# Rotary's loads in GpSimd's queue, and two of the constants' pieces at a time

## The chip, the cores and the metric

The kernel runs on one core of a Trainium2 chip. The metric is the device time in microseconds of one execution, as the median of the runs. The core has the tensor engine (PE, with its weight loads as PEld), the Vector engine (DVE), the Scalar engine (ACT), GpSimd (POOL) and the sync engine (SP). SP, ACT and GpSimd issue DMA transfers, each into a queue of its own.

## What is computed

A decoder trunk of two layers over 1024 tokens of width 1024. Each layer has two mixers beside each other: windowed attention with partial rotary, and a gated linear recurrence (HGRN2). Their outputs are gated, added, projected and added to the stream. Cut to what the change touches:

```python
for layer in range(DEPTH):                     # 2
    h = rms_norm(x, norm_w[layer])
    proj = h @ w_in[layer]                     # (1024, 1024) @ (1024, IN_WIDTH)
    (q, k, v, z_attn, q_h, f_h, i_h, g_h, gate_attn, gate_hgrn) = split(proj)
    q = partial_rope(q.reshape(B, T, 8, 64), positions)    # the first 16 of each head's 64
    k = partial_rope(k.reshape(B, T, 2, 64), positions)
    a = sliding_window_attention(q, k, v, sinks) * silu(z_attn)
    ...                                        # HGRN2: b
    x = x + (sigmoid(gate_attn) * (a @ w_up_attn) + sigmoid(gate_hgrn) * (b @ w_up_hgrn)) @ w_out
return rms_norm(x, final_norm_w)
```

`partial_rope` turns pairs of columns: `x1*cos - x2*sin, x2*cos + x1*sin`. Everything is fp32.

## The kernel before

**Precision and products.** Each fp32 operand is split into a high and a low part. ACT rounds the high part (`whi`, L130, `wh`, L290), the Vector engine subtracts it for the low part (`wlo`, L131, `wl`, L291). A product is three matmuls (lo x hi, hi x lo, hi x hi): L296, L297, L298.

**Pairs.** The columns of `w_in` are worked off in 15 *pairs* m = 0 to 14 (loop at L638, `pair` at L274), each two 128-column blocks, with a Strassen-Winograd scheme that needs seven products of half blocks instead of eight. A pair loads its two weight halves `wr_m_0` and `wr_m_1` (512 KB each, L87, on SP's queue; in the profile both are called `wr`). The Vector engine makes sums and differences from them (`ws`, L282, L283, L285, L286), and ACT and the Vector engine split these (suffixes `_s`, `_t` and, for the first product, `_a`).

PE then does groups of 12 matmuls into two accumulators `pb` and `pc`: `pb` with `_s`, `pc` with `_s`, `pb` with `_t`, `pc` with `_t`, and at the end `pb` with `wl`/`wh`. For the pairs up to 11 (layer 0) or 10 (layer 1) the first product was made earlier; the others have two more groups, with `_a`, in front. Between the groups the Vector engine reads the accumulators out (L307): `pq_12<-pb`, `pq_22<-pc`, `pq_22<-pb`, `pq_12<-pc`, `pq_21<-pb`. The last group overwrites `pb`, so it waits until the third of these, `pq_22<-pb`, has run.

**Weight buffers.** The pool `wraw` has two buffers, so `wr_{m+1}_0` can be issued only after L286 of pair m, the last reader of the first half, and `wr_{m+1}_1` only after L291 of pair m.

**Rotary.** The generator `rotary()` turns five tiles of 128 rows, the keys (n = 0, j = 0) and four of queries (j = 1, 2, 4, 5). It is stepped by `use`, a callback in `pair`, from pair 9 (`TURN`) on. At its first step it loads the tables `cosT` and `sinT` (L604). Each tile is loaded as `y` (512 KB, L610) and once more with the halves of the rotary columns exchanged, as `other` (4 x 32 KB, L615; one buffer for all tiles). Then `y*cos` (L617), `other*sin` (L619), the sum (L620), ACT's high part `yh` (L623) and the low part (L625). GpSimd stores the parts: `ksd` for the keys (8 x 256 KB, L629 and L630), `qsd` for each tile of queries (4 x 256 KB, L633 and L634).

**The constants.** `constants()` makes the rotary tables in four pieces (`tab`, L479 to L493: short steps on the Vector engine, four PE transposes, an ACT copy `tabo` and a store from ACT's queue into `tabs`); `next(consts, None)` at the end of each pair makes one step.

**What sets the order.** Each engine has a queue that it works off in order. A scheduler sets these orders when the kernel is built, from the order of the code and from estimates; on the chip they are fixed. A row behind a waiting one waits too.

Of the kernel before, what the change touches and what calls it, by code (L numbers as in the profile page):

```python
# [28 lines left out]
HALF = 8  # L29
# [11 lines left out]
def trunk_kernel(ctx, tc, x, positions, norm_w, w_in, attn_sinks, hgrn_norm_w, w_up_attn,  # L41
                 w_up_hgrn, w_out, lb_logits, final_norm_w, c_ident, c_side, c_upper, c_diag, c_lev,
                 c_freq, out):
    nc = tc.nc
# [12 lines left out]
    def slot(shape, name, dt=F32):  # L57
        return sp.tile(shape, dt, tag="slot", name=name)
# [330 lines left out]
    tabs = [dp.tile([P, T], F32, name=f"tabs_{i}") for i in range(2)]  # L389
# [115 lines left out]
    consts = constants()  # L505


    for L in range(DEPTH):
# [5 lines left out]
        yd = [dp.tile([P, T], F32, name=f"yd_{L}_{j}") for j in range(6)]  # L514
# [85 lines left out]

        def rotary():
            cosT, sinT = (slot([P, T], f"{n}T_{L}") for n in ("cos", "sin"))
            for t, d in zip((cosT, sinT), tabs):
                nc.sync.dma_start(t, d)  # L604

            o = slot([P, T], f"other_{L}")
            G.memset(o, 0.0)
            for n, j in enumerate((0, 1, 2, 4, 5)):
                y = slot([P, T], f"y_{L}_{j}")
                nc.sync.dma_start(y, yd[j])  # L610
                for r in range(2):
                    for i in range(2):
                        a = r * HD + i * HALF
                        b = r * HD + (1 - i) * HALF
                        nc.sync.dma_start(o[a:a + HALF], yd[j][b:b + HALF])  # L615
                yield
                V.tensor_tensor(out=y, in0=y, in1=cosT, op=ALU.mult)  # L617
                yield
                V.tensor_tensor(out=o, in0=o, in1=sinT, op=ALU.mult)  # L619
                V.tensor_tensor(out=y, in0=y, in1=o, op=ALU.add)  # L620
                yield
                hi = slot([P, T], f"yh_{L}_{j}", F32R)
                S.copy(hi, y)  # L623
                lo = y.bitcast(F32R)
                V.tensor_tensor(out=lo, in0=y, in1=hi.bitcast(F32), op=ALU.subtract)  # L625
                if n == 0:
                    for g, (own, far) in enumerate(((LO, HI), (HI, LO))):
                        for d, u in ((ksd[g][1 - g], (hi, lo)), (ksd[g][g], (lo, hi))):
                            nc.gpsimd.dma_start(d[own], u[0][own].bitcast(F32))  # L629
                            nc.gpsimd.dma_start(d[far], u[1][own].bitcast(F32))  # L630
                else:
                    for d, own, far in ((qsd[n - 1][0], LO, HI), (qsd[n - 1][1], HI, LO)):
                        nc.gpsimd.dma_start(d[own], hi[own].bitcast(F32))  # L633
                        nc.gpsimd.dma_start(d[far], lo[own].bitcast(F32))  # L634
                yield

        turning = rotary()
        for m in range(NPAIR):  # L638
            (c0, r0), (c1, r1) = pairs[m]

            def use(j, a, src, own):
                result(m, *pairs[m][j], a * 512, src, src if own else None)
                if m >= TURN:
                    next(turning, None)
            pair(wi, (c0, c1), parts, hT, f"{L}_{m}", p1s[m] if m < ahead else None, use)
            next(consts, None)
            if m == NPAIR - 2:
                vT, vn = slot([P, T], f"vT_{L}"), [slot([P, NB, P], f"vn_{L}")]
                nc.sync.dma_start(vT, yd[3])
# [470 lines left out]
        for m in range(0, KT, 2):  # L1120
# [5 lines left out]
            for a in range(2):  # L1126
                u, t = u2s[m // 2][a]
# [83 lines left out]
        m = split_a(a11, "s2")  # L1211
# [4 lines left out]
        m = split_a(a21, "s1")  # L1216
# [8 lines left out]
        m = split_a(a12, "s4")  # L1225
# [4 lines left out]
        m = split_a(a11, "s3")  # L1230
# [63 lines left out]
```

## Time and profile before

| | |
|---|---|
| median of 3 runs | 1426.08 us (1421.89 to 1428.8) |
| the profiled execution, its own time | 1425.17 us |
| its span | 1423.4 us |
| PE busy | 1389.6 us (98%) |
| Vector engine busy | 998.8 us (70%) |
| ACT busy | 694.4 us (49%) |
| GpSimd busy | 83.1 us (6%) |
| mean DMA rate | 169 GB/s |

Pair 9, with which rotary begins, starts its matmuls at about 219 us in layer 0 and 911 us in layer 1. A row of a timeline gives start and duration in us, engine, line, operation, output<-input and count; in brackets stands the idle time before and what ended it. A row of the waits view gives what waited, for what, the sum in us, how often and the longest. A row of a window gives each engine's busy time, the granted clock of PE, the share of the DMA engines and GB/s.

### The profile page before, as it was taken

What the parts mean: (1) busy time and instruction counts of PE and PEld (TensorE: products, weight loads), DVE (VectorE), ACT (ScalarE), POOL (GpSimd) and SP (SyncE); (2) the same over time, 40 slices, a digit from 0 to 9 for tenths busy, and PEclk for the clock granted to TensorE, in tenths of its full rate; (3) what the DMA queues carried; (4) which work ended last, traced back from release to release, by engine and by line L of the source; (5) the groups of instructions that cost most, each with busy time, mean ns of one, the idle gap of its engine ahead of it and who ended that gap; (6) DMA issues with size and microseconds to landing.
All of it is one profiled execution on the core that took longest, in us unless ns stands there. A gap on an engine that the chain in (4) does not pass through costs nothing.

```text
span 1423.4 us, 21284 instructions
## 1 busy us (share of the span) xinstructions
PE 1389.6 (98%) x8108; PEld 1125.5 (79%) x8108; DVE 998.8 (70%) x1638; ACT 694.4 (49%) x1386; POOL 83.1 (6%) x141
## 2 busy tenths in 40 slices
PE   8999999999999999999999999989999999999997
PEld 7888777778777787888878788868887778788885
DVE  6867667752755779589976565776347378876998
ACT  8753424343884555313576332334448746443244
POOL 1100001120000001000010000010200000100000
PEclk9999999999999999999999999999999999999999
DMA  9433446787134652671255344576933366329303
GB/s 276 156 126 126 140 156 201 248 268 270 60 119 159 231 189 90 244 264 54 74 198 165 106 130 142 194 222 202 320 123 97 133 213 217 120 62 401 129 0 119
DMA packets 203639, 240.05 MB, mean 169 GB/s; under 512 B 13648, under 2 KB 140112, under 8 KB 203536
## 3 DMA queue, kind: packets, MB, share of 16 engines
q1 hardware_dynamic: 159184, 153.73, 32.8%
q10 hardware_dynamic: 34944, 52.44, 10.2%
q0 software_dynamic: 9408, 32.51, 7.2%
q8 instruction: 64, 1.05, 0.3%
q14 instruction: 39, 0.32, 0.1%
HBM read 160.00 MB, written 78.64 MB: 168 GB/s over the span
## 4 chain that ended last, share of the span: by engine, by line
PE 79%; DVE 8%; DMA 5%; ACT 4%; issue 2%; SPq 1%; ACTq 0%; DVEq 0%
PE pb L296 5%; PE pb L297 5%; PE pb L298 5%; DMA wr<-in_w_in_dram 4%; PE pc L296 3%; PE pc L297 3%; PE pc L298 3%; PE pg L265 2%; PE pg L267 2%; PE pg L266 2%; PE pj_qh L141 2%; PE pj_qh L142 2%; PE av L762 2%; PE pj_qh L143 2%; PE pi L789 2%; PE pi L788 2%
## 5 line engine op out<-in xcount | busy, mean ns | idle before, releaser
L130 ACT CAST whi_s<-ws 128x1024 fp32r<-128x1024 f32 x30 | 31.6, 1052 | 139.6 <-DVE ws L283 120.5
L130 ACT CAST whi_o<-wo 128x1024 fp32r<-128x1024 f32 x20 | 21.1, 1054 | 77.0 <-PE pu_uh L143 35.5
L282 DVE TENSOR_TENSOR ws<-wr 128x512 f32<-128x512 f32 x30 | 20.7, 690 | 52.7 <-DMA wr<-in_w_in_dram 52.7
L532 ACT ACTIVATE pq<-pq 128x512 f32<-128x512 f32 x60 | 37.8, 630 | 31.8 <-DVE pq L307 26.1
L296 PE MATMUL pb<-th,wl 128*128 128x512 f32 x120 | 48.6, 405 | 4.4 <-DVE pq L307 4.3
L141 PE MATMUL pu_ua<-wh_a,wlo_ua 128*128 128x512 f32 x128 | 52.4, 409 | 0.0
L307 DVE TENSOR_TENSOR pq<-pb,p 128x512 f32<-128x512 f32 x46 | 31.7, 689 | 29.2 <-PE pb L298 29.1
L296 PE MATMUL pb<-th,wlo_s 128*128 128x512 f32 x120 | 48.0, 400 | 3.5 <-DVE y L617 3.2
L265 PE MATMUL pg<-hh,wl_p 128*128 128x512 f32 (+1 forms) x128 | 47.8, 375 | 3.0 <-ACT p L269 2.9
L143 PE MATMUL pu_ua<-wh_a,whi_ua 128*128 128x512 f32 x128 | 50.5, 395 | 0.0
L142 PE MATMUL pu_ua<-wl_a,whi_ua 128*128 128x512 f32 x128 | 50.4, 394 | 0.0
L143 PE MATMUL pu_uh<-wh_b,whi_uh 128*128 128x512 f32 x128 | 49.8, 389 | 0.0
L141 PE MATMUL pu_uh<-wh_b,wlo_uh 128*128 128x512 f32 x128 | 49.8, 389 | 0.0
L142 PE MATMUL pu_uh<-wl_b,whi_uh 128*128 128x512 f32 x128 | 49.8, 389 | 0.0
L737 ACT ACTIVATE pr<-pr,mx 128x128 f32<-128x128 f32 x128 | 49.7, 393 | 0.0
L296 PE MATMUL pb<-th,wlo_t 128*128 128x512 f32 x120 | 47.3, 394 | 2.1 <-DVE wlo_t L131 2.1
L296 PE MATMUL pc<-hh,wlo_t 128*128 128x512 f32 x120 | 47.9, 400 | 0.1
L131 DVE TENSOR_TENSOR wlo_t<-ws,whi_t 128x1024 fp32r<-128x1024 f32 x30 | 36.7, 1223 | 15.9 <-ACT whi_t L130 15.9
L297 PE MATMUL pb<-tl,wh 128*128 128x512 f32 x120 | 47.7, 398 | 0.0
L298 PE MATMUL pb<-th,wh 128*128 128x512 f32 x120 | 47.7, 398 | 0.0
L297 PE MATMUL pb<-tl,whi_s 128*128 128x512 f32 x120 | 47.4, 395 | 0.0
L297 PE MATMUL pb<-tl,whi_t 128*128 128x512 f32 x120 | 47.4, 395 | 0.0
(419 smaller groups left out, 4419.1 us busy)
## 6 DMA issues: line engine op xcount, KB each, us to landing
wr<-in_w_in_dram SPq DMA_DIRECT2D x72, 512.0 KB
gd<-pq ACTq DMA_DIRECT2D x79, 256.0 KB
fq<-fq ACTq DMA_DIRECT2D x48, 256.0 KB
wr_p<-in_w_in_dram SPq DMA_DIRECT2D x23, 512.0 KB
x<-in_x_dram SPq DMA_DIRECT2D x16, 512.0 KB
qs<-qsd POOLq DMA_DIRECT2D x16, 512.0 KB, 8.1
u<-gd SPq DMA_DIRECT2D x16, 512.0 KB
ga<-gd SPq DMA_DIRECT2D x16, 512.0 KB
```

The lines of the kernel that those rows point to most:

```text
L130: S.copy(hi, raw)
L131: eng.tensor_tensor(out=lo, in0=raw, in1=hi.bitcast(F32), op=ALU.subtract)
L141: PE.matmul(acc, lhsT=ll, rhs=rh, start=i == 0, stop=False)
L142: PE.matmul(acc, lhsT=lh, rhs=rl, start=False, stop=False)
L143: PE.matmul(acc, lhsT=lh, rhs=rh, start=False, stop=i == n - 1)
L265: PE.matmul(acc, lhsT=wl[:, k], rhs=h[:, t], start=k == 0, stop=False, skip_group_check=q > 0)
L296: PE.matmul(acc, lhsT=wl[:, k], rhs=h, start=start and k == 0, stop=False, skip_group_check=not start)
L297: PE.matmul(acc, lhsT=wh[:, k], rhs=l, start=False, stop=False, skip_group_check=not start)
L298: PE.matmul(acc, lhsT=wh[:, k], rhs=h, start=False, stop=k == 3, skip_group_check=not start)
L307: V.tensor_tensor(out=out, in0=in0, in1=in1, op=ALU.add)
L532: S.activation(d, src, AF.Sigmoid if r < 2 * KT else AF.Silu)
L737: S.activation(pr[:, h], pr[:, h], AF.Exp, bias=mx[:, h:h + 1], accum_out=sm[:, h:h + 1])
```

## The change

Rotary's loads (the tables, `y` and `other`) are issued by GpSimd instead of SP. Each tile's loads stand in the code ahead of the last tile's stores: the new inner function `load` is called for tile 0 before the loop, and for the next tile after the current one's sum. And after pairs 0 and 1 the constants are stepped twice instead of once.

```diff
         def rotary():
             cosT, sinT = (slot([P, T], f"{n}T_{L}") for n in ("cos", "sin"))
-            for t, d in zip((cosT, sinT), tabs):
-                nc.sync.dma_start(t, d)
 
             o = slot([P, T], f"other_{L}")
             G.memset(o, 0.0)
-            for n, j in enumerate((0, 1, 2, 4, 5)):
+
+            def load(j):
                 y = slot([P, T], f"y_{L}_{j}")
-                nc.sync.dma_start(y, yd[j])
+                nc.gpsimd.dma_start(y, yd[j])
                 for r in range(2):
                     for i in range(2):
                         a = r * HD + i * HALF
                         b = r * HD + (1 - i) * HALF
-                        nc.sync.dma_start(o[a:a + HALF], yd[j][b:b + HALF])
+                        nc.gpsimd.dma_start(o[a:a + HALF], yd[j][b:b + HALF])
+                return y
+
+            tiles = (0, 1, 2, 4, 5)
+            for t, d in zip((cosT, sinT), tabs):
+                nc.gpsimd.dma_start(t, d)
+            nxt = load(0)
+            for n, j in enumerate(tiles):
+                y = nxt
                 yield
                 V.tensor_tensor(out=y, in0=y, in1=cosT, op=ALU.mult)
                 yield
                 V.tensor_tensor(out=o, in0=o, in1=sinT, op=ALU.mult)
                 V.tensor_tensor(out=y, in0=y, in1=o, op=ALU.add)
+                if n < 4:
+                    nxt = load(tiles[n + 1])
                 yield
...
             pair(wi, (c0, c1), parts, hT, f"{L}_{m}", p1s[m] if m < ahead else None, use)
-            next(consts, None)
+            for _ in range(1 if m > 1 else 2):
+                next(consts, None)
```

In the changed file the lines are shifted: the loads of the tables are L619, `y` L609, `other` L614, the Vector engine's steps L624, L626, L627 and L634, the stores L638/L639 (`ksd`) and L642/L643 (`qsd`).

In GpSimd's queue, layer 0, this stands before behind the clearing of `other`:

```order
L607 MEMSET other_2123 128x1024
L629 DMA ksd_0_1_161<-yh_0_2232 64x1024
L630 DMA ksd_0_1_161<-y_0_2125 64x1024
L629 DMA ksd_0_0_160<-y_0_2125 64x1024
L630 DMA ksd_0_0_160<-yh_0_2232 64x1024
```

And this after the change:

```order
L605 MEMSET other_2121 128x1024
L619 DMA cosT_2119<-tabs_136 128x1024
L619 DMA sinT_2120<-tabs_137 128x1024
L609 DMA y_0_2125<-yd_0_139 128x1024
L614 DMA other_2121<-yd_0_139 8x1024 x4
L609 DMA y_1_2165<-yd_1_140 128x1024
L614 DMA other_2121<-yd_1_140 8x1024 x4
L638 DMA ksd_0_1_161<-yh_0_2238 64x1024
L639 DMA ksd_0_1_161<-y_0_2125 64x1024
```

The tables and two tiles stand ahead of the first store; each later tile's loads stand ahead of a group of stores.

On the Vector engine, layer 0, from the third readout of pair 9 (`pq_9_22<-pb`) on, before (`y_0` is the tile of keys):

```order
L307 TENSOR_TENSOR pq_9_22_2102<-pb_9_2074,pq_9_22_2102 128x512
L286 TENSOR_TENSOR ws_10_1_2170<-wr_10_0_2165,ws_10_0_2169 128x512
L131 TENSOR_TENSOR wlo_10_s<-ws_10_0_2169,whi_10_s 128x1024
L617 TENSOR_TENSOR y_0_2125<-y_0_2125,cosT_2119 128x1024
L307 TENSOR_TENSOR pq_9_12_2088<-pc_9_2075,pq_9_12_2088 128x512
L131 TENSOR_TENSOR wlo_10_t<-ws_10_1_2170,whi_10_t 128x1024
L307 TENSOR_TENSOR pq_9_21_2159<-pb_9_2074,p_0_8_901 128x512
L291 TENSOR_TENSOR wl_10_2184<-wr_10_1_2167,wh_10_2183 128x512
L619 TENSOR_TENSOR other_2123<-other_2123,sinT_2120 128x1024
```

And after:

```order
L626 TENSOR_TENSOR other_2121<-other_2121,sinT_2120 128x1024
L307 TENSOR_TENSOR pq_9_22_2102<-pb_9_2074,pq_9_22_2102 128x512
L627 TENSOR_TENSOR y_0_2125<-y_0_2125,other_2121 128x1024
L131 TENSOR_TENSOR wlo_10_s<-ws_10_0_2175,whi_10_s 128x1024
L307 TENSOR_TENSOR pq_9_12_2088<-pc_9_2075,pq_9_12_2088 128x512
L286 TENSOR_TENSOR ws_10_1_2176<-wr_10_0_2171,ws_10_0_2175 128x512
L634 TENSOR_TENSOR y_0_2125<-y_0_2125,yh_0_2238 128x1024
L307 TENSOR_TENSOR pq_9_21_2159<-pb_9_2074,p_0_8_901 128x512
L131 TENSOR_TENSOR wlo_10_t<-ws_10_1_2176,whi_10_t 128x1024
L291 TENSOR_TENSOR wl_10_2190<-wr_10_1_2173,wh_10_2189 128x512
```

The keys' rotation, of which only the product with cos stood in this stretch, is now finished in it, its low part (L634) included. `wl_10` is the last reader of `wr_10_1`, so `wr_11_1` follows it.

On the Vector engine, layer 1, around the readout of pair 10 that frees `pb`, before:

```order
L307 TENSOR_TENSOR pq_10_22_8144<-pc_10_8117,p_1_10_7069 128x512
L131 TENSOR_TENSOR wlo_11_a<-wr_11_0_8210,whi_11_a 128x1024
L307 TENSOR_TENSOR pq_10_22_8144<-pb_10_8116,pq_10_22_8144 128x512
L282 TENSOR_TENSOR ws_11_0_8214<-wr_11_1_8212 128x512
L285 TENSOR_TENSOR ws_11_1_8215<-wr_11_0_8210,wr_11_1_8212 128x512
```

And after:

```order
L307 TENSOR_TENSOR pq_10_22_8150<-pc_10_8123,p_1_10_7069 128x512
L131 TENSOR_TENSOR wlo_11_a<-wr_11_0_8210,whi_11_a 128x1024
L282 TENSOR_TENSOR ws_11_0_8214<-wr_11_1_8212 128x512
L307 TENSOR_TENSOR pq_10_22_8150<-pb_10_8122,pq_10_22_8150 128x512
L283 TENSOR_TENSOR ws_11_0_8214<-ws_11_0_8214,wr_11_0_8210 128x512
```

L282, the first reader of `wr_11_1`, now stands ahead of that readout. In layer 0 it stood ahead of it before too (`ws_11_0<-wr_11_1`, then `pq_10_22<-pb`); there L285 has joined it:

```order
L282 TENSOR_TENSOR ws_11_0_2285<-wr_11_1_2283 128x512
L285 TENSOR_TENSOR ws_11_1_2286<-wr_11_0_2281,wr_11_1_2283 128x512
L307 TENSOR_TENSOR pq_10_22_2221<-pb_10_2193,pq_10_22_2221 128x512
L283 TENSOR_TENSOR ws_11_0_2285<-ws_11_0_2285,wr_11_0_2281 128x512
L627 TENSOR_TENSOR y_1_2165<-y_1_2165,other_2121 128x1024
```

These are rows of the changed kernel, whose second tile (`y_1`) is summed right behind.

## The prediction

> **What bounds the kernel now.** The page's first part, the busy time of each engine, comes first:
>
> ```profile
> PE 1389.6 (98%) x8108; PEld 1125.5 (79%) x8108; DVE 998.8 (70%) x1638; ACT 694.4 (49%) x1386; POOL 83.1 (6%) x141
> ```
>
> TensorE (PE) is at work for 1389.6 of 1423.4 us, and the change takes no matmul away. So it can give back only idle PE time and time at a lowered clock. The waits view, for PE and for the tiles of a weight pair, says how much of that there is and who causes it:
>
> ```profile
> PE pb L296 <- DVE pq L307: 4.3, 4, 3.0
> PE pb L296 <- DVE y L617: 3.2, 1, 3.2
> PE pb L296 <- DVE wlo_t L131: 2.1, 1, 2.1
> DVE ws L282 <- DMA wr<-in_w_in_dram: 52.7, 20, 5.6
> ```
>
> Three waits of PE, of 3.0, 3.2 and 2.1 us, are single ones at L296, a matmul of a pair. PE's timeline has each (idle before in brackets), and with it the pitch that follows:
>
> ```profile
> 261.86 0.80 PE L296 MATMUL pb<-th,wl 128*128 128x512 f32 x1 [3.05 <-DVE pq L307]
> 262.45 0.63 PE L297 MATMUL pb<-tl,wh 128*128 128x512 f32 x1
> 262.88 0.63 PE L298 MATMUL pb<-th,wh 128*128 128x512 f32 x1
> ...
> 267.93 0.39 PE L298 MATMUL pb<-hh,whi_a 128*128 128x512 f32 x1
> 268.15 0.39 PE L296 MATMUL pb<-hh,wlo_a 128*128 128x512 f32 x1
> ```
> ```profile
> 946.86 0.63 PE L296 MATMUL pb<-th,wlo_s 128*128 128x512 f32 x1 [3.17 <-DVE y L617]
> ...
> 951.08 0.39 PE L298 MATMUL pb<-th,whi_s 128*128 128x512 f32 x1
> ```
> ```profile
> 956.31 0.47 PE L296 MATMUL pb<-th,wlo_t 128*128 128x512 f32 x1 [2.12 <-DVE wlo_t L131]
> ```
> ```profile
> 260.00:270.00 10.00, 8.14 (x24) 6.47 (x25) 9.66 (x13) 4.71 (x6) 0.00 (x0) 0.66 0.55 193
> ```
>
> After 3.05 us idle the matmuls start 0.43 us apart (262.45, 262.88) instead of 0.22 (267.93, 268.15), until 267.93: the last row, a 10-us window, has a granted clock of 0.66 (the number before 0.55). 14 matmuls took 6.07 us (261.86 to 267.93) instead of 14 x 0.227 = 3.18, so this stall cost 3.05 + 2.9 = 6.0 us. After 946.86 there are 11 matmuls in 4.22 us instead of 2.5: 3.17 + 1.7 = 4.9 us. The third, of 2.12 us, I take with 1.2 of slow clock, less than the second's 1.7: 3.3. All three lie where rotary works, in pairs 11 (layer 0) and 10 and 11 (layer 1): 14.2 us, 1.0% of the time, is about all that the change can win.
>
> What is late? The chain of waits has the transfers behind these stalls, and one undisturbed one (start, us):
>
> ```profile
> 206.03 4.71 DMA wr<-in_w_in_dram
> ```
> ```profile
> 249.92 10.67 DMA wr<-in_w_in_dram
> ```
> ```profile
> 926.83 12.31 DMA wr<-in_w_in_dram
> ```
> ```profile
> 945.75 8.56 DMA wr<-in_w_in_dram
> ```
>
> A wr is one 512-KB half of a pair's weights. Undisturbed it takes 4.7 us, here 8.6 to 12.3. GpSimd's timeline shows what stands beside it, the eight stores of rotated keys (ksd):
>
> ```profile
> 240.72 0.54 POOL L629 DMA_DIRECT2D ksd<-yh  x1 [27.67 <-ACT yh L623]
> 241.98 0.55 POOL L630 DMA_DIRECT2D ksd<-y  x1 [0.72 <-DVE y L625]
> ...
> 245.16 0.55 POOL L630 DMA_DIRECT2D ksd<-yh  x1
> ```
> ```profile
> 922.86 0.55 POOL L630 DMA_DIRECT2D ksd<-y  x1 [0.79 <-DVE y L625]
> ```
>
> They are 8 x 256 KB. The DMA view of the stretch 926.9 to 931, right after the wr of 926.83 was issued, shows who is served (q0 is GpSimd's queue, q1 SP's, q10 ACT's):
>
> ```profile
> q0 software_dynamic: 245, 0.80, 78.6%
> q10 hardware_dynamic: 148, 0.27, 21.4%
> q1 hardware_dynamic: 1, 0.00, 0.0%
> ```
>
> SP's queue moved one packet in 4.1 us. So the stalls come from a burst of stores in GpSimd's queue ahead of a weight load, not from SP being held up at its issue: the weight load at 249.92 went out as soon as its buffer was free, behind L291.
>
> ```profile
> 249.21 0.68 DVE L291 TENSOR_TENSOR wl<-wr,wh 128x512 fp32r<-128x512 f32 x1
> ```
>
> **The change part by part.** *SP's queue without rotary's loads.* 16 rows a layer leave it. Since SP issued that load within 0.03 us of its release (249.21 + 0.68 = 249.89), an emptier SP wins nothing there: 0.
>
> *The rotation of tile 0 moves forward.* Its loads go out as soon as the tables are written, and the Vector engine's order places its last steps earlier (L627, the add, ahead of wlo_10_s; L634, the low half that releases seven of the eight stores, ahead of pq_9_21). With these rows of before
>
> ```profile
> 228.30 0.69 DVE L307 TENSOR_TENSOR pq<-pb,pq 128x512 f32<-128x512 f32 x1 [0.23 <-PE pb L298]
> ...
> 235.01 0.68 DVE L307 TENSOR_TENSOR pq<-pb,p 128x512 f32<-128x512 f32 x1
> 235.78 0.69 DVE L291 TENSOR_TENSOR wl<-wr,wh 128x512 fp32r<-128x512 f32 x1
> ...
> 240.46 1.23 DVE L625 TENSOR_TENSOR y<-y,yh 128x1024 fp32r<-128x1024 f32 x1 [0.52 <-ACT yh L623]
> ```
>
> I walk layer 0, a 512-wide step at 0.60 us pitch (235.78 to the next at 236.39) and a 1024-wide one at 1.14: pq_9_22 at 228.30, L627 to 230.1, wlo_10_s to 231.2, pq_9_12 and L286 to 232.4, L634 to 233.6. The second ksd store goes out at 233.6 instead of 241.98, the last at about 233.6 + 6 x 0.54 = 236.8. The load wr_11_1 goes out behind wl_10: 233.6 + 0.60 (pq_9_21) + 1.14 (wlo_10_t) + 0.69 = 236.0. Before, it went out at 236.5, 4.2 us ahead of the first store. Now it has the burst just ahead of it, as the loads of 926.83 and 249.92 had. That is the cost of this part.
>
> *What wr_11_1's lateness costs in layer 0.* By the like case (12.31 us from issue) it lands at 248.3; counted from the second store (922.86 to 939.14 is 16.3 us) at 249.9; I take 249. Its readers L282 and L285 now stand ahead of pq_10_22<-pb, which frees the accumulator for the pair's last 12 matmuls; from that step to PE it took 0.74 us:
>
> ```profile
> 261.12 0.68 DVE L307 TENSOR_TENSOR pq<-pb,pq 128x512 f32<-128x512 f32 x1
> ```
> ```profile
> 244.42 0.39 PE L296 MATMUL pb<-th,wl 128*128 128x512 f32 x1
> ```
> ```profile
> 935.37 0.39 PE L296 MATMUL pb<-th,wl 128*128 128x512 f32 x1
> ```
>
> 249.0 + 0.60 + 0.60 + 0.74 = 250.9 against 244.42: 6.5 us of idle PE, and 2.9 of slow clock as at 261.86, 9.4 together. In return the burst is over when pair 12's halves come, and the 6.0 us at 261.86 go. Layer 0: +3.4. The unknown is the landing. Undisturbed it is 236.0 + 4.7 = 240.7, which makes no stall (the limit is 244.42 - 1.94 = 242.5, 6.5 us after issue); by the load of 249.92, which ended at 260.6, 18.6 us after its second store, it is 252.2. So layer 0 is worth -6 to +7. I take the late value because the load of 926.83 is the nearest case, with a burst just ahead and one packet in 4.1 us.
>
> The Trainium skill ("DMA: Bandwidth & Descriptors", section "Queues, rings and completion order") has another rule: each DMA engine goes round the queues that have work and gives each a packet in turn. By it the load would have had its share from the start; the row of q1 above disagrees, and only the share of later moments could agree. The sum by the rule is rival C's.
>
> *Layer 1.* The same walk from
>
> ```profile
> 918.93 0.69 DVE L307 TENSOR_TENSOR pq<-pb,pq 128x512 f32<-128x512 f32 x1 [0.29 <-PE pb L298]
> ...
> 921.35 1.22 DVE L625 TENSOR_TENSOR y<-y,yh 128x1024 fp32r<-128x1024 f32 x1
> ```
>
> gives L634 to 924.8 (919.5 + two 1.14-us steps + three of 0.60 + 1.22) and wr_11_1 at 928.4, where L624 of the next tile stands ahead of wl_10 as well. So here the burst comes 2 us later than before (L625 began at 921.35) and the load 1.6 us later: the same collision. It lands at 940.7 to 941.2. What is new is that L282 stands ahead of pq_10_22<-pb, behind which it stood before; so PE's last 12 matmuls of pair 10 wait too: 941 + 0.60 + 0.74 = 942.3 against 935.37, 6.9 us, with 2.3 of slow clock (between 1.7 and 2.9) 9.2. Gone are 4.9 and 3.3: 8.2. Of the stall at 956.31 something comes back, since L282 of pair 12 now stands ahead of wlo_11_t and pair 12's second half meets tile 1's stores: 0 to 3.3, I take 1.6. Layer 1: +2.6 (-8 to +7, from the same two ends).
>
> *The constants' pieces two by two.* Each of the four pieces (4 transposes, 4 short steps on the Vector engine, a copy and a store on ACT) goes two pairs earlier. The last one is on the Vector engine at
>
> ```profile
> 220.45 0.17 DVE L483 COPY tab<-sins 128x32 f32<-128x32 f32 x1
> ```
> ```profile
> PEld tt L490 <- issue: 1.6, 4, 0.5
> ```
>
> and comes, two pairs of 60 matmuls at 0.227 us earlier, near 193. The four held up TensorE's weight loads by 1.6 us together (0.5 at most); another place can double that or spare it. 0, between -1.6 and +1.6.
>
> *Sum.* 0 + 3.4 + 2.6 + 0 = +6.0 us. The profiled execution took 1425.17 us (its span, 1423.4, and 1.8 around it), so 1431.2; the median of the three runs is 0.9 higher, so 1432.1, as 1432.
>
> **The rivals.** *B, the burst meets nothing (faster).* If wr_11_1 lands within 6.5 us in layer 0 and 5.6 us in layer 1 (935.37 - 0.74 - 0.60 less 928.4), no new stall comes and the old ones go: -6.0 - 8.2 + 1.6 = -12.6, so 1413. For it: rotary's own 512-KB loads no longer stand in the weights' queue, and the store queue starts on a less crowded stretch. Against it: the load of 926.83 had no such load just ahead of it and still took 12.3.
>
> *C, even turns.* If the queues shared the DMA engines evenly, a load that takes 4.71 us undisturbed would take about twice that beside one busy queue, 9.4, a little more than the 8.56 of the load at 945.75. Gaps: 236.0 + 9.4 + 1.94 - 244.42 = 2.9, and 928.4 + 9.4 + 1.34 - 935.37 = 3.8, with 1.7 of slow clock each: 10.1 against 14.2 gone and 1.6 that come back, -2.5, so 1424 (1421 to 1427; a full collision in one layer alone falls there too). This is the skill's rule above worked out; against it stands the packet count of q1.
>
> *D, the stalls add up (slower).* The whole rotation runs on one queue now, loads ahead of stores: a late tile 1 releases its stores and the loads of tile 2 just when pair 12's halves are asked for, and then a stall like those of before follows each new one. Place: L282 of pair 12, ahead of pq_11_22<-pc in layer 0 and of wlo_11_t in layer 1. Price: 9.4 + 9.2 new, with half to all of the 14.2 of before kept: +11.5 to +18.6, 1438 to 1445. It decides, in layer 1, when pair 12's second half takes over 5.8 us: it goes out about 1.5 us after pair 10's last matmul (0.60 for pq_10_21, 0.69 for wl_11), wlo_11_t is due 4 x 12 x 0.227 = 10.9 us after it, and 0.60 + 0.60 + 1.14 + 1.22 lie between landing and its end.
>
> That the rotation is not earlier at all is excluded by the order for the Vector engine, as long as the tables and y_0 are there; the tables' last piece, near 193, is 35 us ahead of the first add (L627).
>
> **How the numbers follow.** A measurement of this kernel can tell about 0.5% (7.1 us) from no change. My case A (a stall in each layer, 1427 to 1437) gets 0.42, of which 0.26 lie under 1433.2 and 0.16 over it; B 0.25, all faster; C 0.15, within 0.5%; D 0.18, slower. So faster 0.25, same 0.26 + 0.15 = 0.41, slower 0.16 + 0.18 = 0.34. The range goes from B's 1413 to 1441, in the middle of D, which leaves out about half of D and the lower part of B. The likeliest case's own range is 1427 to 1437.
>
> **What would show it.** Right: ksd stores from about 232 to 237 and 923 to 929; wr_11_1 landing 11 to 14 us after its issue; a gap of 5 to 8 us at the last 12 matmuls of pair 10 in both layers, at half clock behind it; none at 261.86. Wrong: wr_11_1 within 6 us (then B), or gaps in pairs 11 and 12 as large as those in pair 10 (then D). If gaps of that kind are absent and the time is still not under 1420, the loss lies in a place that I did not look at.

## The result and the profile after

| | before | after the change |
|---|---|---|
| median | 1424.2 us (4 runs) | 1447.01 us (4 runs, 1445.03 to 1450.12) |
| ratio | | 1.0163 [1.0133, 1.0194] |
| profiled execution (span) | 1425.17 us (1423.4) | 1446.37 us (1444.6) |

The changed kernel is slower by 1.6%, 22.8 us. The forecast was 1432 us and the range ended at 1441, so the time lies outside it, in the direction of case D and past D's upper end, 1445.

The page's first part shows the same work in a longer span: PE is busy for 0.1 us more than before, ACT and the Vector engine for the same. Only GpSimd has more, with 54 more instructions, the loads.

```profile
PE 1389.7 (96%) x8108; PEld 1126.1 (78%) x8108; DVE 998.4 (69%) x1638; ACT 695.0 (48%) x1386; POOL 110.9 (8%) x195
```

So the loss is idle PE time. The waits view says whose (sum, number, longest):

```profile
PE pb L296 <- DVE pq L307: 18.3, 6, 9.3
PE pc L296 <- DVE pq L307: 6.1, 4, 2.9
PE pb L296 <- DVE wlo_a L131: 6.1, 2, 3.9
DVE ws L282 <- DMA wr<-in_w_in_dram: 83.3, 27, 11.1
```

The last row stands behind most of the others, as the places below and the experiments show: the Vector engine waits at L282 for a weight half for 83.3 us instead of 52.7, and up to 11.1 us instead of 5.6. PE's timeline has the gaps, first those that the prediction named (the last 12 matmuls of pair 10, layer 0 and layer 1, and the place of the old gap at 261.86):

```profile
253.54 0.80 PE L296 MATMUL pb<-th,wl 128*128 128x512 f32 x1 [9.35 <-DVE pq L307]
...
269.74 0.39 PE L296 MATMUL pb<-th,wl 128*128 128x512 f32 x1
...
956.50 0.80 PE L296 MATMUL pb<-th,wl 128*128 128x512 f32 x1 [7.19 <-DVE pq L307]
```

and then those that it did not: pairs 6 and 7 of layer 1 (which it did not look at), and pair 13 of layer 0 (where the kernel before has 1.11 us, at 301.53) and 12 of layer 1.

```profile
307.81 0.50 PE L296 MATMUL pb<-hh,wlo_a 128*128 128x512 f32 x1 [2.15 <-DVE wlo_a L131]
...
888.27 0.50 PE L296 MATMUL pc<-hh,wlo_t 128*128 128x512 f32 x1 [2.89 <-DVE pq L307]
...
904.34 0.50 PE L296 MATMUL pc<-hh,wlo_t 128*128 128x512 f32 x1 [2.17 <-DVE pq L307]
...
999.60 0.80 PE L296 MATMUL pb<-hh,wlo_a 128*128 128x512 f32 x1 [3.91 <-DVE wlo_a L131]
```

The same matmul, found at the same place in PE's order of both timelines, tells what each place cost in all, slow clock included. How far the changed kernel is behind:

| matmul | before, us | after, us | behind |
|---|---|---|---|
| layer 0, pair 9, `pc` with `_s` | 222.64 | 222.27 | -0.4 |
| pair 10, last group | 244.42 | 253.54 | +9.1 |
| pair 11, last group | 261.86 | 269.74 | +7.9 |
| pair 12, `pa` with `_a` | 270.21 | 275.18 | +5.0 |
| first of attention | 341.27 | 348.27 | +7.0 |
| layer 1, pair 6, `pb` with `_t` | 874.71 | 882.50 | +7.8 |
| pair 6, `pc` with `_t` | 877.44 | 888.27 | +10.8 |
| pair 7, `pc` with `_t` | 891.22 | 904.34 | +13.1 |
| pair 10, `pb` with `_t` | 929.93 | 943.57 | +13.6 |
| pair 10, last group | 935.37 | 956.50 | +21.1 |
| pair 12, `pb` with `_s` | 971.67 | 987.37 | +15.7 |
| pair 13, `pa` with `_a` | 988.38 | 1009.44 | +21.1 |

(`pa` is the accumulator of the second group that the late pairs have in front.) The stall in pair 10 and what it gives back later leave +5.4 in layer 0 (from -0.4 to +5.0) and +2.1 in layer 1 (13.6 to 15.7), 7.5 together; +2.0 come behind it in layer 0 (5.0 to 7.0). Two more places are nearly as large: +5.3 in pairs 6 and 7 of layer 1 (7.8 to 13.1), for which the prediction had nothing, and +5.4 around pair 12 of layer 1 (15.7 to 21.1), for which it had little. The rest are small steps: 0.8 in layer 1 ahead of pair 6 and 0.5 between pairs 7 and 10.

The keys' stores and the load behind them, `wr_11_1`, stand in GpSimd's timeline and in the chain of waits, layer 0:

```profile
233.47 0.57 POOL L638 DMA_DIRECT2D ksd<-yh  x1
234.97 0.55 POOL L639 DMA_DIRECT2D ksd<-y  x1 [0.94 <-DVE y L634]
...
238.16 0.55 POOL L639 DMA_DIRECT2D ksd<-yh  x1
```
```profile
237.04 14.53 DMA wr<-in_w_in_dram
```
```profile
942.94 12.19 DMA wr<-in_w_in_dram
```

The load is issued in the middle of the burst in layer 0 and takes 14.5 us, at the end of the burst in layer 1 and takes 12.2. Behind the last store GpSimd sends the third tile's `y` (512 KB, at 238.99 and 943.52) as well. In pairs 6 and 7 of layer 1 it is rotary's own loads that stand beside the weights:

```profile
877.15 0.54 POOL L619 DMA_DIRECT2D cosT<-tabs  x1 [1.61 <-DVE wlo_t L131]
878.25 0.54 POOL L619 DMA_DIRECT2D sinT<-tabs  x1 [0.56 <-DVE pq L307]
891.57 0.54 POOL L609 DMA_DIRECT2D y<-yd  x1 [12.78 <-DVE wlo_s L131]
...
894.09 0.57 POOL L609 DMA_DIRECT2D y<-yd  x1
```

1 MB (two tables) just ahead of the weight half issued at 878.6, and 1.1 MB (two tiles, one `other`) ahead of that of 895.4. The reader L282, on the Vector engine, in these two pairs before and after:

```profile
875.37 0.69 DVE L282 TENSOR_TENSOR ws<-wr 128x512 f32<-128x512 f32 x1 [2.48 <-DMA wr<-in_w_in_dram]
...
889.27 0.69 DVE L282 TENSOR_TENSOR ws<-wr 128x512 f32<-128x512 f32 x1 [2.74 <-DMA wr<-in_w_in_dram]
```
```profile
886.32 0.69 DVE L282 TENSOR_TENSOR ws<-wr 128x512 f32<-128x512 f32 x1 [5.65 <-DMA wr<-in_w_in_dram]
...
902.39 0.69 DVE L282 TENSOR_TENSOR ws<-wr 128x512 f32<-128x512 f32 x1 [4.93 <-DMA wr<-in_w_in_dram]
```

Before, the Vector engine already waits 2.5 to 2.7 us there while PE still has work; behind L282 stands the readout L307 that frees `pc`. So the margin was used up: 3.2 us more of waiting are 2.9 us of idle PE (888.27). The rows of the Vector engine and of ACT stand in the same order here before and after; only the loads are new. The DMA view of the changed kernel from 878.6 to 882, behind the issue of that weight half, shows GpSimd's queue (q0) with most of the time of the DMA engines and SP's (q1) with 31 packets; before, SP's queue moved 676 packets (37.3%) in the 3.4 us behind the same issue, at 870.85.

```profile
q0 software_dynamic: 198, 0.74, 66.8%
q1 hardware_dynamic: 31, 0.02, 1.5%
```

### The profile page after: what moved, and what is told of

It is laid out like the page before. It is cut to its first block, busy times and chain, and to the rows that moved or that the text cites. A ratio compares the mean times of both kernels' runs of the same rounds, so it can differ in the third digit from the quotient of the medians.

```text
span 1444.6 us, 21260 instructions
## 1 busy us (share of the span) xinstructions
PE 1389.7 (96%) x8108; PEld 1126.1 (78%) x8108; DVE 998.4 (69%) x1638; ACT 695.0 (48%) x1386; POOL 110.9 (8%) x195
## 4 chain that ended last, share of the span: by engine, by line
PE 76%; DMA 8%; DVE 7%; ACT 4%; issue 4%; POOL 0%; SPq 0%; DVEq 0%; ACTq 0%; POOLq 0%
DMA wr<-in_w_in_dram 5%; PE pb L296 4%; PE pb L298 4%; PE pb L297 4%; PE pc L296 3%; PE pc L298 3%; PE pc L297 3%; PE pg L265 2%; PE pg L267 2%; PE pg L266 2%; PE pj_qh L141 2%; PE pj_qh L142 2%; PE av L772 2%; PE pj_qh L143 2%; PE pu_uh L141 2%
## 5 line engine op out<-in xcount | busy, mean ns | idle before, releaser
L282 DVE TENSOR_TENSOR ws<-wr 128x512 f32<-128x512 f32 x30 | 20.8, 692 | 83.3 <-DMA wr<-in_w_in_dram 83.3
L130 ACT CAST whi_o<-wo 128x1024 fp32r<-128x1024 f32 x20 | 21.1, 1054 | 77.0 <-PE pu_uh L143 35.5
L307 DVE TENSOR_TENSOR pq<-pb,p 128x512 f32<-128x512 f32 x46 | 31.7, 690 | 30.1 <-PE pb L298 29.9
L298 PE MATMUL pc<-hh,whi_t 128*128 128x512 f32 x120 | 46.9, 391 | 0.0
L297 PE MATMUL pc<-hl,whi_t 128*128 128x512 f32 x120 | 46.9, 391 | 0.0
```

The lines of the kernel that those rows point to most:

```text
L130: S.copy(hi, raw)
L297: PE.matmul(acc, lhsT=wh[:, k], rhs=l, start=False, stop=False, skip_group_check=not start)
L298: PE.matmul(acc, lhsT=wh[:, k], rhs=h, start=False, stop=k == 3, skip_group_check=not start)
L307: V.tensor_tensor(out=out, in0=in0, in1=in1, op=ALU.add)
```

## The experiments

**The theories.** T, called T2 in its later form: what delays a weight half is the amount of data that stands in GpSimd's queue when it is issued (the keys' 2 MB in a burst, or 1 MB of rotary's loads). In its first, strong form T also said that GpSimd's queue is served ahead of SP's, so that the same bytes from SP cost little. The expectations of e1 to e3 set a rival R against it (the loads in GpSimd's queue are the whole loss, the stores cost nothing), those of e4 to e8 a rival B (the bytes count, in whichever queue). The rivals that mattered later: R2, the changed order on the Vector engine makes the gaps (a reader of a late half stands ahead of a readout); and D, in the last two runs, the length of the rows that a transfer is cut into. Some of the expectations number the pairs of layer 1 that are called 6, 7 and 12 here one or two higher. The row that each run is judged by is given with it.

**e1: the constants alone.** The kernel before with the last part of the diff.

```diff
-            next(consts, None)
+            for _ in range(1 if m > 1 else 2):
+                next(consts, None)
```

> The kernel before with the constants two by two, rotary's loads still in SP's queue. In layer 0 the keys' rotation then stands one pair earlier on the Vector engine, as in the changed kernel; in layer 1 it stands as before. Theory T (what is put into GpSimd's queue just ahead of a weight load holds that load up by 5 to 10 us, wherever it falls): the keys' stores fall ahead of wr_11_1 in layer 0, so PE waits 6 to 9.5 us at the last 12 matmuls of pair 10 there, the 3-us gap in pair 11 goes, layer 1 is unchanged: 1428 to 1433 us. Rival R (the loads in GpSimd's queue are the whole loss, the stores are not): no gap over 4 us in pair 10, 1421 to 1427.

Measured: 1427.77 us against 1423.38, ratio 1.0032 [1.0017, 1.0046]. The stall moves in layer 0 as in the changed kernel, at half the size; layer 1 stays as it was.

```profile
248.94 0.80 PE L296 MATMUL pb<-th,wl 128*128 128x512 f32 x1 [4.46 <-DVE pq L307]
...
284.77 0.79 PE L296 MATMUL pb<-hh,wlo_a 128*128 128x512 f32 x1 [3.36 <-DVE wlo_a L131]
```

So the constants decide when layer 0's rotation comes, and that alone costs 4.4 us: the stall of pair 10, the old one of pair 11 gone, a new one of 3.4 us two pairs later. The place was expected, the size was not (4.5 us, not 6 or more). R, with no gap over 4 us, is missed too.

**e2: the loads alone.** The changed kernel with one step of the constants after every pair.

```diff
-            for _ in range(1 if m > 1 else 2):
-                next(consts, None)
+            next(consts, None)
```

> The changed kernel with the constants stepped once per pair, so rotary's loads in GpSimd's queue alone. In layer 0 the low half of the keys (L634) stands behind wl_10, so wr_11_1 is issued ahead of seven of the eight stores. T: no gap over 4 us in pair 10 of layer 0; layer 1 as in the changed kernel (gaps of 2 to 3 us in pairs 7 and 8, 7 us in pair 10, 4 us in pair 13): 1434 to 1442. R: all of the loss, 1443 to 1449.

Measured: 1441.8 us, 1.0148 [1.0112, 1.0184] (its profiled execution took 1450.12, so its gaps are read with care). The two times add up to the whole change, 4.4 + 18.4 = 22.8 us, but the places do not: at the first matmul of attention in layer 0, e1 is 3.6 us behind the kernel before, e2 10.7 and the changed kernel 7.0. In layer 1 the gaps are nearly those of the changed kernel (2.93 us at 891.34, 7.64 at 960.12; in pair 7 0.94 instead of 2.17). In layer 0 the expectation of no gap over 4 us failed: pair 10 has one of 5.41 (239.19, for `wlo_s`) and one of 6.95 (253.49). Without the constants' part the rotation there comes later, and meets another wait: L626 waits 1.82 us for the table `sinT` (at 230.90), ahead of pair 10's `wlo_s`. R's 1443 to 1449 is missed by 1.2 us.

**e3: the loads early, but from SP.** The changed kernel with SP for all of rotary's loads.

```diff
-                nc.gpsimd.dma_start(y, yd[j])
+                nc.sync.dma_start(y, yd[j])
...
-                        nc.gpsimd.dma_start(o[a:a + HALF], yd[j][b:b + HALF])
+                        nc.sync.dma_start(o[a:a + HALF], yd[j][b:b + HALF])
...
-                nc.gpsimd.dma_start(t, d)
+                nc.sync.dma_start(t, d)
```

> The changed kernel with rotary's loads issued by SP again, still each ahead of the last tile's stores, constants two by two. T: the gaps in pairs 6 to 9 of layer 1 (6 us in all) and most of that in pair 13 go, since GpSimd's queue is empty there; the keys' stores still stand ahead of wr_11_1, so the gaps in pair 10 of both layers stay (5 to 9 us each): 1430 to 1440. R: no gap over 4 us in pair 10, 1421 to 1427.

Measured: 1433.42 us, 1.0078 [1.0053, 1.0102], 10.0 us more than before. The gaps in pairs 6 and 7 of layer 1 are gone; the one at the end of pair 10 stays, smaller. In layer 0, where 5 us or more were expected, it is 2.04 (250.60), and another of 3.05 stands ahead of it (236.02; e12 comes back to it). In layer 1 it is 4.92, and 0.92 is the largest ahead of it:

```profile
867.22 0.50 PE L296 MATMUL pc<-hh,wlo_t 128*128 128x512 f32 x1 [0.92 <-DVE pq L307]
...
944.86 0.79 PE L296 MATMUL pb<-th,wl 128*128 128x512 f32 x1 [4.92 <-DVE pq L307]
```

So of the 22.8 us 12.8 go when the loads go back to SP, and 10.0 stay with the earlier place of loads and rotation. In layer 0 the Vector engine's order differs between the two builds as well; in pairs 6 and 7 of layer 1 it is the same, so there it is the loads alone. SP's own timeline shows what the queue does here. SP works off seven weight halves first, and the tables and `y_0` go out right behind the last of them, where nothing is due soon:

```profile
859.55 42.65 SPq L87 DMA_DIRECT2D wr<-in_w_in_dram  x7
902.29 0.53 SPq L619 DMA_DIRECT2D cosT<-tabs  x1
902.88 0.50 SPq L619 DMA_DIRECT2D sinT<-tabs  x1
903.43 0.79 SPq L609 DMA_DIRECT2D y<-yd  x1
```

(The half issued at 901.83 is waited for 2.64 us, as elsewhere, and the next goes out at 915.05.) GpSimd, with nothing else to do, sent them at 877.15, 1.5 us ahead of a weight half. SP's order had kept them apart.

**e4: the keys' stores from ACT.** The kernel before.

```diff
-                            nc.gpsimd.dma_start(d[own], u[0][own].bitcast(F32))
-                            nc.gpsimd.dma_start(d[far], u[1][own].bitcast(F32))
+                            nc.scalar.dma_start(d[own], u[0][own].bitcast(F32))
+                            nc.scalar.dma_start(d[far], u[1][own].bitcast(F32))
```

> The kernel before with the keys' eight stores issued by ACT instead of GpSimd. T: ACT's queue does not hold SP's back as GpSimd's does; the waits of L282 and wlo_12_a for the weights after the burst shrink to under 2 us and the gaps of 3 us in pairs 11 and 10/11 go: 1410 to 1419. Rival B (it is the 2 MB of stores, in whichever queue): the gaps stay within 1.5 us of what they were, 1421 to 1430.

Measured: 1427.5 us, 1.003 [1.0018, 1.0042]. The weights are on time now: the longest wait at L282 is 3.1 us.

```profile
DVE ws L282 <- DMA wr<-in_w_in_dram: 44.4, 20, 3.1
```

But ACT is held up by issuing the stores, and PE waits for ACT's share of the weights' split:

```profile
250.78 1.15 ACT L532 ACTIVATE pq<-pq 128x512 f32<-128x512 f32 x2 [7.49 <-DMA ksd<-y]
```
```profile
255.76 0.80 PE L296 MATMUL pb<-th,wlo_s 128*128 128x512 f32 x1 [8.43 <-DVE wlo_s L131]
```

T was right on the weights and wrong on the time, which it put under 1420. The run does not tell the queue from the pace: ACT issued the eight stores over 9.6 us in layer 0 (239.93 to 249.54), GpSimd over 4.4 (240.72 to 245.16).

**e5, e6, e7: one load beside each weight half.** The kernel before with one more 512-KB load, of data that nothing uses, in each of the pairs 4 to 8 of layer 1 (behind L287), from GpSimd (e5), ACT (e6) or SP (e7). A one-column copy on the Vector engine ahead of it sets its time. The lines shift: L282 is L284.

```diff
+        if probe:
+            V.tensor_copy(junk[:, 0:1], l1[:, 0, 0, 0:1].bitcast(F32))
+            nc.gpsimd.dma_start(junk, probe[0])
...
+            probe[:] = [yd[0]] if L == 1 and 4 <= m <= 8 else []
```

> The kernel before with one 512-KB load added in each of pairs 4 to 8 of layer 1 (an old projection tile into a scratch tile, released by wlo_t, about 2 us ahead of the next pair's second weight half), issued by GpSimd. Before, L282 of the next pair waits 2.5 to 2.8 us for that half. T: GpSimd's transfer is served first, the five waits grow by 1.5 us or more, to 4 to 6 us, and PE gets gaps of 1 to 3 us: 1426 to 1436. Rival B (bytes, not the queue): the same growth in this run and in the next two, within 0.5 us.

> The same five loads, issued by ACT. T: ACT's queue shares with SP's, and the waits of L282 grow by 1 us at most, to 2.5 to 3.8 us; 1421 to 1428. B: as with GpSimd.

> The same five loads, issued by SP, where they stand between the two weight halves. They take their turn in one queue, so the second half is 512 KB later, at the 250 GB/s or so of this stretch 2 us: waits of L282 of 3.5 to 5 us; 1423 to 1432. Both theories expect about this; it is the scale for the other two.

Measured, against 1422.54 us: e5 1427.2, 1.0038 [1.0018, 1.0058]; e6 1425.98, 1.0023 [1.0009, 1.0036]; e7 1429.26, 1.0048 [1.0028, 1.0069]. The wait of L284 in the first of the pairs, from GpSimd and from SP:

```profile
844.26 0.69 DVE L284 TENSOR_TENSOR ws<-wr 128x512 f32<-128x512 f32 x1 [4.08 <-DMA wr<-in_w_in_dram]
```
```profile
850.15 0.69 DVE L284 TENSOR_TENSOR ws<-wr 128x512 f32<-128x512 f32 x1 [3.04 <-DMA wr<-in_w_in_dram]
```

Over the five pairs the wait is 3.40 to 4.08 us with the load on GpSimd (mean 3.78) and 2.86 to 4.17 on SP (3.40), against 2.48 to 2.80 before, about 2.7. (On ACT, 0.41 to 3.04, but there a readout stands ahead of L284, so the rows do not compare.) A load of 512 KB costs 1.1 us of waiting through GpSimd and 0.7 through SP, and the times of the three runs are not told apart by their intervals. T had expected 1.5 or more for GpSimd; its strong form falls, and B's "within 0.5 us" holds for these two queues. The Trainium skill ("DMA: Bandwidth & Descriptors", section "Issuing engines are not separate DMA queues") has it so: transfers that SP, ACT and GpSimd start run on the same 16 DMA engines and interleave. By that the move of the loads to another queue could win nothing by itself, and it won nothing; what it cost, it cost by when they go out (e3). What is left of T is the amount that stands ahead: 1.1 us for 512 KB, 3.2 for 1 MB at 886.32.

**e8: the keys' stores in four slices each.** The kernel before; 32 stores of 64 KB in place of 8 of 256 KB, same queue, same bytes.

```diff
-                            nc.gpsimd.dma_start(d[own], u[0][own].bitcast(F32))
-                            nc.gpsimd.dma_start(d[far], u[1][own].bitcast(F32))
+                            for c in range(0, T, 256):
+                                nc.gpsimd.dma_start(d[own, c:c + 256], u[0][own, c:c + 256].bitcast(F32))
+                                nc.gpsimd.dma_start(d[far, c:c + 256], u[1][own, c:c + 256].bitcast(F32))
```

> The kernel before with each of the keys' eight stores cut into four column slices of 256, 32 stores of 64 KB from GpSimd; same bytes, but issued over some 17 us instead of 4.5. T (the backlog in GpSimd's queue is served ahead of the weights): the backlog stays small, the weight halves of pairs 11 and 12 land within 8 us, the gaps of 3 us in pair 11 of layer 0 and at the end of pair 10 of layer 1 shrink under 1.5 us: 1412 to 1420. B: the bytes compete as before, 1421 to 1428.

Measured: 1418.53 us, 0.997 [0.9958, 0.9982]. The three gaps that the prediction began with are gone; a new one of 4.27 us stands at 278.44, where the queries' stores, still whole, come.

**e9: the queries' stores sliced as well.** As e8, and the same loop around the two `qsd` stores (L633, L634).

> The kernel before with the keys' and the queries' stores cut into four column slices each (64 KB, from GpSimd). Theory T2 (what counts is the bytes that stand in GpSimd's queue in one go ahead of a load): the gap of 4.3 us that came up in pair 13 of layer 0 with the keys alone sliced shrinks under 2.5, the others stay away: 1411 to 1417. Rival (that gap has another cause, or slices that drag on hold up the buffers): as with the keys alone or slower, 1417 to 1424.

Measured: 1415.22 us against 1423.47, ratio 0.9945 [0.9931, 0.9958]: the fastest version here, faster than both kernels of the change. The order on the Vector engine in pairs 9 to 12 is that of the kernel before, so nothing but the stores has changed there. The largest gap in the pairs is 1.51 us. The DMA view of 922.5 to 926.6, in the middle of the keys' stores of layer 1 and behind the issue of a weight half, answers to the one packet in 4.1 us that the prediction quoted:

```profile
q1 hardware_dynamic: 915, 0.46, 39.7%
q0 software_dynamic: 144, 0.31, 29.9%
q10 hardware_dynamic: 144, 0.26, 18.2%
```

**e10: the changed kernel with all stores sliced** (the same two loops).

> The changed kernel (loads in GpSimd's queue) with all stores cut into four slices. T2: the gaps of 9.4 and 7.2 us in pair 10 shrink under 4; those in pairs 7 and 8 of layer 1 (2.9 and 2.2), which come from loads that stand there ahead of any store, stay: 1428 to 1438. Rival R2 (the order of the Vector engine's rows makes the gaps in pair 10, not the burst): they stay over 5 us, 1442 to 1450.

Measured: 1430.65 us, 1.0051 [1.0033, 1.0068]. The Vector engine's order in pairs 9 and 10 is the changed kernel's, yet the stall of 9.35 us in pair 10 of layer 0 is 1.15 us, and the one of layer 1 is gone; the same load takes 6.33 us instead of 14.53. (With the stores cut, the third tile's `y` also goes out later, at 252.09.)

```profile
244.38 0.50 PE L296 MATMUL pb<-th,wl 128*128 128x512 f32 x1 [1.15 <-DVE pq L307]
```
```profile
236.08 6.33 DMA wr<-in_w_in_dram
```

R2 falls for this gap: with its order left in place, the gap goes when the burst goes. The gaps of rotary's loads, which are still whole, stay (3.30 us in pair 6 and 1.39 in pair 7):

```profile
883.37 0.50 PE L296 MATMUL pc<-hh,wlo_t 128*128 128x512 f32 x1 [3.30 <-DVE pq L307]
```

**e11: the loads sliced too.** As e10, with the tables and `y` loaded in four column slices.

```diff
-                nc.gpsimd.dma_start(y, yd[j])
+                for c in range(0, T, 256):
+                    nc.gpsimd.dma_start(y[:, c:c + 256], yd[j][:, c:c + 256])
...
-                nc.gpsimd.dma_start(t, d)
+                for c in range(0, T, 256):
+                    nc.gpsimd.dma_start(t[:, c:c + 256], d[:, c:c + 256])
```

> The run before, with the loads of the tables and of y cut into four column slices as well (128 KB, rows of 1 KB instead of 4 KB). The two tables are still 1 MB in GpSimd's queue within some 4 us. T2: the gaps in pairs 7 and 8 of layer 1 stay over 1.5 us. Rival D (it is the length of the rows: short ones let SP's queue have its turns): both under 1 us.

Measured: 1425.37 us, 1.0017 [1.0004, 1.003]. The 3.30 us become 1.13, and the 1.39 become 0.50. T2 had both over 1.5, D both under 1; neither is met.

```profile
874.17 0.50 PE L296 MATMUL pc<-hh,wlo_t 128*128 128x512 f32 x1 [1.13 <-DVE pq L307]
```

The slices also spread the issue of the tables, over 4.3 us, so size and pace are not told apart here.

**e12: e3 with all stores sliced** (loads early, from SP).

> The changed kernel's code with its loads back on SP, constants two by two, and all stores cut into four slices. T2: no burst is left in GpSimd's queue; no gap over 2.5 us in pairs 6 to 14 of either layer: 1410 to 1418. Rival (being early is itself the cost): gaps in pair 10 as with whole stores (2 to 5 us), 1426 to 1434.

Measured: 1419.51 us, 0.9971 [0.9961, 0.9981]. The rival's 1426 to 1434 is out; T2's 1410 to 1418 is missed by 1.5 us, and a gap over its 2.5 us stays, in pair 10 of layer 0:

```profile
236.19 0.50 PE L296 MATMUL pb<-th,wlo_s 128*128 128x512 f32 x1 [3.05 <-DVE wlo_s L131]
```

No weight half is late at this one, for L282 waits for nothing. Four steps of rotary's arithmetic (L626, L627, L624 and L634, 1.2 us each) stand on the Vector engine ahead of pair 10's `wlo_s`:

```profile
225.62 1.22 DVE L626 TENSOR_TENSOR other<-other,sinT 128x1024 f32<-128x1024 f32 x1
...
229.75 0.68 DVE L282 TENSOR_TENSOR ws<-wr 128x512 f32<-128x512 f32 x1
...
233.78 1.22 DVE L634 TENSOR_TENSOR y<-y,yh 128x1024 fp32r<-128x1024 f32 x1
234.91 1.22 DVE L131 TENSOR_TENSOR wlo_s<-ws,whi_s 128x1024 fp32r<-128x1024 f32 x1
```

The order there is e3's, which has the same 3.05 us. So a part of what being early costs is the place of the arithmetic itself; no run moved it alone.

The runs with sliced stores price the change again: 4.3 us for the earlier place (e12 over e9) and 11.1 for the queue of the loads (e10 over e12).

**e13 and e14: cut by rows instead of columns.** A slice of 256 columns has rows of 1 KB. e13 is the kernel before with every store cut into four pieces of 16 rows of 4 KB, 64 KB each as in e9. e14 is the changed kernel with this, and with tables and `y` loaded 32 rows at a time.

```diff
-                            nc.gpsimd.dma_start(d[own], u[0][own].bitcast(F32))
-                            nc.gpsimd.dma_start(d[far], u[1][own].bitcast(F32))
+                            for c in range(0, HD, 16):
+                                k = slice(own.start + c, own.start + c + 16)
+                                e = slice(far.start + c, far.start + c + 16)
+                                nc.gpsimd.dma_start(d[k], u[0][k].bitcast(F32))
+                                nc.gpsimd.dma_start(d[e], u[1][k].bitcast(F32))
```

> The kernel before with all stores cut into four again, but by rows (16 rows of 4 KB each, 64 KB) instead of columns (64 rows of 1 KB). Same bytes, same count of stores, same pace of issue as in the run with all stores sliced (1415). T2 (what counts is how much stands in GpSimd's queue at once): no gap over 1.6 us in pairs 10 to 13, 1412 to 1419. D (what counts is the length of the rows): the gaps of 3 us in pair 11 of layer 0 and at the end of pair 10 of layer 1 are back, 1420 to 1427.

> The changed kernel with all its stores and the loads of tables and y cut by rows (loads of 32 rows of 4 KB, 128 KB). T2: as with everything cut by columns, the gaps in pairs 7 and 8 of layer 1 about 1.1 and 0.5 us, time 1420 to 1428. D: both as with whole loads, 3.3 and 1.4, time 1428 to 1440.

Measured: e13 1428.49 us against 1421.94, 1.0037 [1.0024, 1.005]. In the pairs it does at first what e9 does: the old gaps are gone, and PE is 6.3 us ahead of before at 270 us. So for these gaps the pieces count and not their rows, and D falls. But T2 is missed as well, in the time and with a gap of 1.91 us in pair 12 of layer 0 (276.90). PE is 2.0 us ahead at the end of layer 0's pairs and 3.3 behind where those of layer 1 come: e13 loses its time behind the pairs. One thing that changes there is the load that reads the keys back for attention. It stands in GpSimd's queue behind the last stores, in e13 and in e9:

```profile
314.62 1.12 POOL L684 DMA_DIRECT2D ks<-ksd  x2 [0.64 <-DMA qsd<-y]
```
```profile
304.44 1.13 POOL L680 DMA_DIRECT2D ks<-ksd  x2
```

It goes out 10.2 us later. That this load costs the time is not shown: PE works on without a pause up to the first matmul of attention, only in another order, with 36 more matmuls ahead of it (at 349.66 instead of 341.27). What is seen is 2.3 us by 337.53, where PE waits 1.24 and 0.76 us for the next weights (`wh_i`, `wl_i`); the rest was not looked into. e14 took 1525.68 us, 1.0728 [1.0696, 1.0761]. Its order on the engines is another one, with waits of 7.3 us for `wlo_s` in several pairs, which were not looked into. Of its gaps in pairs 6 and 7 of layer 1, the first, 2.31 us, lies between T2's 1.1 and D's 3.3, and the second, 1.60, above D's 1.4. For the loads, row length against amount stays open.

## Why the prediction was wrong

**What bounds the kernel: right.** Weight halves that are late behind a burst in GpSimd's queue. e8 to e10 show it: with the same bytes, queue and order on the Vector engine, but in pieces of 64 KB, the halves are on time and these stalls go.

**An emptier SP wins nothing: right** as far as it goes, and e5 to e7 show why: a load costs the weights nearly as much in one queue as in another. (27 rows a layer left SP's queue, two tables, five `y` and twenty `other`, and not 16.)

**The keys' stores meet `wr_11_1`: right in place and about right in size.** Forecast in layer 0: stores from 232 to 237, load issued at 236.0, 13 us, a stall of 6.5 us, +3.4 in all. Measured: 233.5 to 238.7, 237.04, 14.53 us, 9.35 us, +5.4. In layer 1 forecast 928.4 and 12.3 to 12.8 us; measured, 13.6 us later because of the delay so far, 942.94 and 12.19, with +2.1 in place of +2.6. Together 7.5 us against 6.0. The gap at 261.86 went, as said. That layer 1 comes out so near is partly luck, since two misses cancel: the stall cost more than forecast (10.2 us, from 13.6 to 23.8 in pair 11, against 9.2), and the 1.6 us that were to come back at 956.31 did not. One thing in that part was put in the wrong place: the two old stalls of layer 1 (946.86 and 956.31) both lie in pair 11.

**The step that failed: what rotary's own loads do in the queue they move to.** The prediction priced leaving SP's queue (0) and never the arrival in GpSimd's: its sum has no term for it, and rival B even counted the move as a gain. The mechanism that it had just shown for the stores, data ahead of a weight half, was not applied to the loads. In layer 1 they come as 1 MB and 1.1 MB, in pairs 6 and 7, ahead of rotary's arithmetic (from 923 us), and there PE had next to no margin: +5.3 us. e3 takes these gaps away with the Vector engine's order there unchanged, since SP sends the loads behind its weight halves; e11 cuts the larger from 3.3 to 1.1 us. Of the 15 us by which the trace lies behind the sum (21.1 against 6.0), these are 5.3; the later tiles, below, are 7.4, the size of the stall in pair 10 is 1.5. SP's queue was no hindrance to be cleared; its order was the schedule.

**Also undersized: the later tiles.** Case D named them as a rival and gave it 0.18; the sum took 1.6 us, for pair 11. Measured are +2.0 in layer 0 and +5.4 around pair 12 of layer 1. In e10, with sliced stores, the two matmuls of the table there are 2.8 and 2.6 us behind, where the changed kernel goes from 15.7 to 21.1: these 5.4 us go when the stores are cut. They go as well when the loads go back to SP and the stores stay whole: in e3 the two are 6.1 and 6.7 behind. So it takes both in one queue, which is what D said. Of D's bill the old stalls kept were wrong (they went), a new one later was right, one pair behind the place that D named: the L282 that waits is pair 13's (3.76 us, at 993.64), ahead of `wlo_13_a`.

**The constants' pieces: at nothing as pieces, not as a clock.** e1 makes them worth 4.4 us, by setting when layer 0's rotation starts. The prediction had this under the rotation's move; e1's stall there, 4.46 us, is under its 6.5, and the 9.35 needed the loads as well.

**What stays open.** Why layer 0 pays so little for the loads beside pairs 6 and 7. There they stand beside first weight halves (issued at 185.70 and 200.12, right behind L286, and landing after 6.1 and 5.7 us), while the second halves, for which L282 waits, go out at 191.86 and 207.02 and land after 5.0 and 4.7 us; in layer 1 it is the second halves that meet the loads. The pairs of layer 0 also take longer, 14.1 and 15.2 us before the change (157.44, 171.54 and 186.70, the last groups of pairs 4 to 6) against 13.7 in layer 1, which would leave PE's waits more room. No run tried either. How much of the earlier place's cost is rotary's arithmetic on the Vector engine (3.05 us idle in e3 and e12). Whether slices help by their size or because GpSimd, waiting for its own earlier slices, spreads them out: the runs always changed both. And the row length for the loads.

## What to carry to other kernels

Moving a transfer to an idle queue does not make it free, and a busy queue's order may be what kept it out of the way: price it against the load that is due next, and ask how much of that load's wait is already used up (here 2.5 us of waiting on the Vector engine with nothing left for PE). Where a large store that nobody waits for stands beside a small load that the bound engine needs, cut the store into pieces before moving anything; the cut alone was worth 0.55% here, the move cost 1.6%. Then look at what comes behind the pieces, since e13 lost behind the pairs what it had won in them.

## What the runs showed of the hardware

- Eight stores of 256 KB in GpSimd's queue let SP's queue move 1 packet in 4.1 us; in e9, with slices of 64 KB, it moved 915 in such a stretch. The Trainium skill ("DMA: Bandwidth & Descriptors", section "Rules for kernel authors") advises to put small transfers together, with mostly overhead under 64 KB. Here 64-KB pieces instead of 256 made the kernel faster (0.9945); what counted is what the large ones stood in front of.
- ACT was slow to issue the keys' stores in e4, and its arithmetic stood still meanwhile (7.49 us at 250.78): up to 1.68 us for one, against 0.55 on GpSimd.

```profile
247.82 1.68 ACTq L629 DMA_DIRECT2D ksd<-y  x1
```

- In the places seen, the price of what stands ahead rose faster than its amount: 1.1 us of waiting for one 512-KB load, 3.2 for 1 MB, and with the 2 MB of keys (and another 512-KB `y` behind them) a weight half lands after 12.2 and 14.5 us instead of 4.7. The three come from different places of the program, and the last is a landing and not a wait, so the steps between them are rough.
